# The fourth sum of x later, a PSUM bank for the last token's first half, and one weight remainder made on VectorE

## The chip, the cores and the metric

The kernel runs on one core of a Trainium2 chip. The metric is the device time of one execution in microseconds (us); before the change it is 1440.09 us, the median of three runs from 1439.65 to 1441.46.

## The reference

Two layers of a gated block over 512 tokens of width 1024, in float32. What matters here is the second half of each layer, the SwiGLU:

```python
hn = rmsnorm(x, norm2_g[i])
gate, up = jnp.split(hn @ w_ffn_in[i], 2, axis=-1)      # FFN_HIDDEN = 2816
x = x + (jax.nn.silu(gate) * up) @ w_ffn_out[i]
```

The first half of a layer (one input projection, a pool mixer, differential attention, the output projection) is not changed.

## The kernel before

**Precision by splitting.** Every operand of a product is split into a high part (a cast to float32r on ScalarE, `whi`, `xqh` and so on) and a low part (the value minus the high part, on VectorE: `wlo`, `xql`). A product is three matmuls: high by high (L291 in the SwiGLU), low of x by high of the weight (L293), high of x by low of the weight (L294).

**SwiGLU by seven products.** The 22 blocks of 128 hidden columns are made in eleven pairs (`Ffn(f0)` for f0 = 0, 2, ... 20). A pair needs the product of x (two halves of 512 rows of the width, two halves of 256 tokens) with its gate and up columns, and does it with seven products of quarters instead of eight (`p(n)`, n = 1 to 7, each 24 matmuls of 256 columns). The x side is seven quarters or sums of quarters, made once a layer by `Quarters`: `b11`, `b21`, `b22` are plain quarters, `t1` to `t4` are sums. Of the tiles, `xq` holds b11, b21, b22 and t1, `xr` holds t2 and t3, `xt` holds t4. The sixth product reads t2, the fifth t1, the seventh t3, the third b22, the fourth t4.

**Where the quarters come from.** For each block t of 128 tokens, `normed` makes the normed rows `xs`; `turn` transposes them on TensorE, eight 128x128 blocks, four to a PSUM bank of the pool `tr` (two banks). For t = 0 and 1, `put` copies and splits. For t = 2 and 3 it makes t1 = tvs[0] − r11 (L389), t2 = tvs[1] − t1 (L390), t3 = b22 − tvs[0] (L395) and t4 = r21 − t2 (L398), each with a split (ScalarE's cast L195, VectorE's remainder L196).

**The weight side.** A piece of weights is 128x1024 (512 KB), loaded through SyncE's queue into one of seven `raw` buffers. `parts` splits it. With a piece number it does so without VectorE: ScalarE writes the high part (L233) and −src into the low part (L234), and GpSimd issues a DMA that adds the same weights from memory to it (L235): an accumulating transfer. A pair's sums of weights are made by VectorE in `sums` (L774, L775, L776, L785; `ws` and `raw`).

**The order of the stage.** `ffn_start` takes the first two pairs (`early`): both first products, both second products (while the last two token blocks are transposed), both pairs' `sums`, then `rest` of each: products 6, 5, 7, 3, 4, with the sums on VectorE that put the pieces together (`cqn` L816, `cta` L824, `cpwl` L828, `cal` L830, `cpwh` L836) and `swiglu` (the tanh `th` on ScalarE, L728, its products on VectorE, L729 and L730, then the split into `fh`, `fl`). From the third pair on `ffn_in` does the same for one pair: products 1, 6, 5, 2, 7, 3, 4. The pairs' first and second products gather in a bank of pool `sc`, 6, 7 and 5, 3 in banks of `mm`, the fourth in a bank of `tr`.

The order in which the instructions stand on each engine, and which of a pool's buffers a tile gets, is set when the program is built, by a scheduler that works through the whole program; each engine then runs its instructions in that order. A small edit can so move instructions elsewhere.

Of the kernel before, what the change touches and what calls it, by code (L numbers as in the profile page):

```python
# [22 lines left out]
NT = S // P  # L23
# [84 lines left out]
def trunk_kernel(  # L108
# [12 lines left out]
    nc = tc.nc  # L121
# [10 lines left out]
    def tr_ps():  # L132
        return ps.tile([P, 512], F32, name="tr", tag="tr", bufs=2)

    oy = ps.tile([P, 2, VD], F32, name="oy", tag="oy")
# [57 lines left out]
    def split(hi, lo, src):  # L193

        ins = nc.scalar.copy(hi, src)  # L195
        nc.vector.tensor_sub(lo, src, hi.bitcast(F32))  # L196
        return ins
# [17 lines left out]
    def loaded():  # L215

        i = at[0]
        at[0] += 1
        raw = sb.tile([P, 4, VD], F32, name="raw", tag="raw", bufs=RAWS)
        nc.sync.dma_start(raw.rearrange("p a b -> p (a b)"), wts[i])  # L220
        return i, raw

    def tiles(x):
        return [x[:, k, :] for k in range(x.shape[1])]

    def parts(src, piece_no=None):

        hi = sb.tile([P, 4, VD], F32R, name="whi", tag="whi", bufs=SPLITS)
        lo = sb.tile([P, 4, VD], F32R, name="wlo", tag="wlo", bufs=SPLITS)
        if piece_no is None:  # L230
            split(hi, lo, src)
        else:
            nc.scalar.copy(hi, src)  # L233
            nc.scalar.activation(lo, src, AF.Copy, scale=-1.0)  # L234
            nc.gpsimd.dma_start(lo.rearrange("p a b -> p (a b)"), wts[piece_no], accum_op=ALU.add)  # L235
        return tiles(hi), tiles(lo)
# [23 lines left out]
    def later(delay, what):  # L260
        heapq.heappush(waiting, (clock[0] + delay, count[0], what))
        count[0] += 1
# [36 lines left out]
    def transpose(dst, src):  # L299
        nc.tensor.transpose(dst, src, ident)  # L300
        clock[0] += 2 * P

    def rsqrt_mean(ss, n, width, times=(1.0,), eps=None):

        r = sb.tile([P, width], F32, name="r", tag="r", bufs=4)
        part = width // len(times)
        for i, f in enumerate(times):
            cs = slice(i * part, (i + 1) * part)
            e = EPS / (f * f) if eps is None else eps[i]
            nc.vector.tensor_scalar(r[:, cs], ss[:, cs], 1.0 / (n * f * f), e, op0=ALU.mult, op1=ALU.add)  # L310
        nc.gpsimd.tensor_tensor(r, r, mhalf[:, :width], op=ALU.pow)  # L311
        return r

    def small(name, width=1):
        return sb.tile([P, width], F32, name=name, tag=name, bufs=4)
# [3 lines left out]
    def need(*keys):  # L319
        run_due(lambda: all(k in ready for k in keys))  # L320
# [7 lines left out]
    def normed(key, t, xh, xl, g, into=None):  # L328

        xs = sb.tile([P, D], F32, name="xs", tag="mj", bufs=2)  # L330
        ss = small("ss")
        nc.scalar.activation(xs, res[t], AF.Square, accum_out=ss)
        r = rsqrt_mean(ss, D, 1)
        for half in range(2):
            cs = slice(half * 512, (half + 1) * 512)
            nc.vector.scalar_tensor_tensor(xs[:, cs], res[t][:, cs], r, g[half], op0=ALU.mult, op1=ALU.mult)  # L336

        def turn():
            tvs = []
            for half in range(2):  # L340
                tp = tr_ps()
                for i in range(4):
                    k = half * 4 + i
                    transpose(tp[:, i * P:(i + 1) * P], xs[:, k * P:(k + 1) * P])
                tv = tp.rearrange("p (k c) -> p k c", k=4)
                tvs.append(tv)
                if into is None:
                    ks = slice(half * 4, half * 4 + 4)
                    copied = split(xh[:, ks, t * P:(t + 1) * P], xl[:, ks, t * P:(t + 1) * P], tv)
            if into is not None:  # L350
                copied = into(t, tvs)
            ready.add((key, t))
            return copied

        later(NORM_WAIT, turn)

    class Quarters:


        def __init__(self):  # L360
            four = [sb.tile([P, 4, 4, VD], F32R, name="xq" + p, tag="x" + p) for p in "hl"]
            two = [sb.tile([P, 2, 4, VD], F32R, name="xr" + p, tag="qk", bufs=2) for p in "hl"]
            one = [sb.tile([P, 4, VD], F32R, name="xt" + p, tag="v", bufs=2) for p in "hl"]
            self.b11, self.b21, self.b22, self.t1 = ([x[:, i] for x in four] for i in range(4))
            self.t2, self.t3 = ([x[:, i] for x in two] for i in range(2))
            self.t4 = one
            self.raw = {}

        def put(self, t, tvs):

            cs = slice(t % 2 * P, (t % 2 + 1) * P)

            def out(to, src):
                return split(to[0][:, :, cs], to[1][:, :, cs], src)

            if t < 2:
                for half, to in ((0, self.b11), (1, self.b21)):
                    raw = sb.tile([P, 4, P], F32, name="xw", tag=f"pr{half}", bufs=2)
                    nc.scalar.copy(raw, tvs[half])
                    self.raw[t, half] = raw  # L380
                    last = out(to, raw)
                return last
            r11, r21 = self.raw[t - 2, 0], self.raw[t - 2, 1]

            def temp(tag, bufs):
                return sb.tile([P, 4, P], F32, name="xd", tag=tag, bufs=bufs)

            t1, t2, t3, t4 = temp("us", 2), temp("us", 2), temp("ta", 2), temp("ta", 2)
            nc.vector.tensor_sub(t1, tvs[0], r11)  # L389
            nc.vector.tensor_sub(t2, tvs[1], t1)  # L390
            out(self.t2, t2)
            out(self.t1, t1)
            b22 = temp("up", 2)
            nc.scalar.copy(b22, tvs[1])
            nc.vector.tensor_sub(t3, b22, tvs[0])  # L395
            out(self.b22, b22)
            out(self.t3, t3)
            nc.vector.tensor_sub(t4, r21, t2)  # L398
            return out(self.t4, t4)

    def new_xT():
        xh = sb.tile([P, KD, S], F32R, name="xh", tag="xh")
# [110 lines left out]
    for layer in range(L):  # L513
# [232 lines left out]
        class Ffn:  # L746
# [15 lines left out]
            def gate_in(self, *tags):  # L762
                self.sets[2] = parts_in(self.r12, *tags)

            def sums(self, a12=False):

                _, r21 = loaded()
                n22, r22 = loaded()
                if a12:
                    self.gate_raw(1)  # L770
                s1 = sb.tile([P, 4, VD], F32, name="ws", tag="raw", bufs=RAWS)
                if a12:
                    self.gate(0, self.n11)
                nc.vector.tensor_add(s1, r21, r22)  # L774
                nc.vector.tensor_sub(r21, self.r11, r21)  # L775
                nc.vector.tensor_sub(self.r11, s1, self.r11)  # L776
                self.sets[6] = parts(self.r11)
                if not a12:
                    self.sets[4] = parts(r22, n22)
                self.sets[5] = parts(s1)  # L780
                if a12:
                    self.gate(1, self.n12)
                else:
                    self.sets[7] = parts(r21)
                nc.vector.tensor_sub(self.r12, self.r12, self.r11)  # L785
                if a12:
                    self.sets[7] = parts(r21)
                self.sets[3] = parts(self.r12)
                if a12:
                    self.sets[4] = parts(r22, n22)  # L790
                self.to = hidden_pair(self.f0)
                for i in range(2):
                    hidden[self.f0 + i] = self.to[i]

            def temp(self, tag, bufs=1):
                return sb.tile([P, 2, VD], F32, name="c" + tag, tag=tag, bufs=bufs)
# [42 lines left out]
        quarters, early, last_merged = [], [], []  # L839
# [44 lines left out]
        def ffn_in(f0):  # L884
            x = Ffn(f0)
            x.gate_raw(0)
            x.sums(True)
            x.first()
            x.rest(True)

        def ffn_start():
            need(*((f"h{layer}", t) for t in range(2)))
            for x in early:
                x.first()
            for x in early:
                x.second()
            need(*((f"h{layer}", t) for t in range(2, 4)))
            for x in early:
                x.sums()
            for x in early:  # L900
                x.rest()

# [14 lines left out]
        for r, (f0, f1) in enumerate(ROUNDS):  # L917
            for f in range(f0, f1, 2):
                if f >= 4:
                    ffn_in(f)  # L920
                elif not f:
                    ffn_start()
                if r and f == f0:
                    ffn_out(*ROUNDS[r - 1], False)
# [58 lines left out]
```

## Time and profile before

| | |
|---|---|
| median of three runs | 1440.09 us |
| profiled execution, in all | 1441.58 us |
| its span (first to last instruction) | 1439.8 us |
| TensorE busy | 1428.5 us, 99% |
| VectorE busy | 989.7 us, 69% |
| ScalarE busy | 688.8 us, 48% |
| accumulating transfers (GpSimd's queue) | 62 of 512 KB, median 7.9 us from issue to landing |
| loads of weight pieces (SyncE's queue) | 244 of 512 KB, median 4.3 us |
| granted TensorE clock | 0.999 |

In the profile PE is TensorE, DVE VectorE, ACT ScalarE, POOL GpSimd and SP SyncE. A row of the timeline has the start in us from the span's start, the duration, the engine, the line of the code, the operation, what it writes and reads, and in brackets the engine's idle time before it with what ended it. A row of waits has the waiting instruction, what it waited for, the total in us, how often, and the longest. The first layer's SwiGLU begins near 374 us, the second's about 715 us later. The matmuls of 256 columns start 0.12 us apart; the 0.28 us of their rows overlap.

### The profile page before, as it was taken

The numbers are of one execution on the slowest core, as the hardware profiler recorded it, in microseconds if no ns is written. First come the engines' busy times: TensorE is split into PE (matmuls) and PEld (weight loads), VectorE is DVE, ScalarE is ACT, GpSimd is POOL, SyncE is SP. The second block draws the span as 40 slices with busy tenths as digits, with TensorE's granted clock in tenths as the row PEclk, the third lists the DMA queues.
The fourth block names the chain that finished last, engine by engine and source line by source line (L and its number), as shares of the span: only waits on it lengthen the run. The fifth ranks groups of instructions, "written<-read, shape, count | busy, mean of one in ns | idle before, by whom it ended". The sixth has DMA issues, their size and how long they took to land.

```text
span 1439.8 us, 21587 instructions
## 1 busy us (share of the span) xinstructions
PE 1428.5 (99%) x8375; PEld 1260.5 (88%) x8375; DVE 989.7 (69%) x1837; ACT 688.8 (48%) x1311; POOL 115.2 (8%) x146
## 2 busy tenths in 40 slices
PE   9999999999999999999999999999999999999999
PEld 7878888888999899989888888888889998999897
DVE  7768677677898548737576686665769975587462
ACT  6544343444666346526355443434446662464350
POOL 1010000000011001000010001001000100010000
PEclk9999999999999999999999999999999999999999
DMA  9212231224268357628322132222422783575361
GB/s 361 97 59 70 95 108 59 89 78 120 74 161 208 116 140 176 195 47 236 113 92 78 59 117 79 76 74 73 130 60 79 184 217 107 132 190 163 83 152 59
DMA packets 49782, 173.02 MB, mean 120 GB/s; under 512 B 5648, under 2 KB 6544, under 8 KB 49680
## 3 DMA queue, kind: packets, MB, share of 16 engines
q1 hardware_dynamic: 39456, 137.02, 28.8%
q0 software_dynamic: 8928, 32.51, 12.5%
q10 hardware_dynamic: 1296, 2.11, 0.6%
q8 instruction: 66, 1.08, 0.3%
q14 instruction: 36, 0.29, 0.1%
HBM read 169.52 MB, written 2.10 MB: 119 GB/s over the span
## 4 chain that ended last, share of the span: by engine, by line
PE 91%; issue 3%; DVE 3%; DMA 2%; POOL 0%; ACT 0%; POOLq 0%
PE mm L279 19%; PE mm L281 19%; PE mm L280 19%; PE mm L291 5%; PE mm L293 5%; PE mm L294 5%; PE sc L294 2%; PE sc L293 2%; PE sc L291 2%; PE tr L300 2%; DMA wlo<-in_wts 1%; PE tr L294 1%; PE tr L293 1%; PE tr L291 1%; DVE xs L336 1%
## 5 line engine op out<-in xcount | busy, mean ns | idle before, releaser
L195 ACT CAST whi<-raw 128x1024 fp32r<-128x1024 f32 (+1 forms) x223 | 232.4, 1048 | 206.4 <-issue 118.7
L196 DVE TENSOR_TENSOR wlo<-raw,whi 128x1024 fp32r<-128x1024 f32 (+1 forms) x223 | 269.5, 1215 | 82.0 <-ACT whi L195 79.2
L279 PE MATMUL mm<-whi,xh 128*128 128x512 f32 x480 | 192.4, 401 | 0.0
L281 PE MATMUL mm<-whi,xl 128*128 128x512 f32 x480 | 187.7, 391 | 0.0
L280 PE MATMUL mm<-wlo,xh 128*128 128x512 f32 x480 | 187.4, 390 | 0.0
L718 DVE TENSOR_TENSOR res<-mm,res 128x512 f32<-128x512 f32 (+1 forms) x97 | 65.9, 683 | 116.0 <-PE mm L281 116.0
L281 PE MATMUL mm<-whi,fl 128*128 128x512 f32 (+1 forms) x358 | 138.5, 387 | 0.0
L279 PE MATMUL mm<-whi,fh 128*128 128x512 f32 (+1 forms) x358 | 138.3, 387 | 0.0
L280 PE MATMUL mm<-wlo,fh 128*128 128x512 f32 (+1 forms) x358 | 138.2, 387 | 0.0
L311 POOL TENSOR_TENSOR r<-r,mhalf 128x1 f32<-128x1 f32 (+1 forms) x76 | 59.1, 778 | 635.8 <-DVE r L310 572.9
L281 PEld LDWEIGHTS mm<-whi,xl 128*128 128x128 f32 x480 | 90.1, 188 | 19.5
L279 PEld LDWEIGHTS mm<-whi,xh 128*128 128x128 f32 x480 | 90.2, 188 | 16.8
L280 PEld LDWEIGHTS mm<-wlo,xh 128*128 128x128 f32 x480 | 90.4, 188 | 16.3
L235 POOL DMA_DIRECT2D wlo<-in_wts x62 | 54.3, 877 | 616.1 <-ACT wlo L234 278.0
L279 PE MATMUL mm<-xh,whi 128*128 128x512 f32 x256 | 102.1, 399 | 0.0
L281 PE MATMUL mm<-xh,wlo 128*128 128x512 f32 x256 | 99.9, 390 | 0.0
L291 PE MATMUL mm<-xrh,whi 128*128 128x256 f32 x352 | 99.8, 283 | 0.2
L280 PE MATMUL mm<-xl,whi 128*128 128x512 f32 x256 | 99.8, 390 | 0.0
L293 PE MATMUL mm<-xrl,whi 128*128 128x256 f32 x352 | 99.7, 283 | 0.0
L291 PE MATMUL mm<-xqh,whi 128*128 128x256 f32 x352 | 99.6, 283 | 0.0
L293 PE MATMUL mm<-xql,whi 128*128 128x256 f32 x352 | 99.6, 283 | 0.0
L294 PE MATMUL mm<-xqh,wlo 128*128 128x256 f32 x352 | 99.6, 283 | 0.0
(211 smaller groups left out, 3519.9 us busy)
## 6 DMA issues: line engine op xcount, KB each, us to landing
raw<-in_wts SPq DMA_DIRECT2D x244, 512.0 KB, 4.3
wlo<-in_wts POOLq DMA_DIRECT2D x62, 512.0 KB, 7.9
xr<-in_x_t SPq DMA_DIRECT2D x4, 512.0 KB, 7.7
res<-in_x SPq DMA_DIRECT2D x4, 512.0 KB, 8.7
pwr<-in_pool_w ACTq DMA_DIRECT2D x8, 256.0 KB, 2.7
out<-res SPq DMA_DIRECT2D x7, 256.0 KB, 2.0
g<-in_gains SPq DMA_DIRECT2D x6, 256.0 KB, 3.1
hg<-in_rows SPq DMA_DIRECT2D x4, 128.0 KB, 7.0
```

What stands on the lines that cost most here:

```text
L195: ins = nc.scalar.copy(hi, src)
L196: nc.vector.tensor_sub(lo, src, hi.bitcast(F32))
L235: nc.gpsimd.dma_start(lo.rearrange("p a b -> p (a b)"), wts[piece_no], accum_op=ALU.add)
L279: nc.tensor.matmul(acc, lhsT=ah, rhs=bh, start=i == 0, stop=False)
L280: nc.tensor.matmul(acc, lhsT=ah, rhs=bl, start=False, stop=False)
L281: nc.tensor.matmul(acc, lhsT=al, rhs=bh, start=False, stop=i == n - 1)
L291: nc.tensor.matmul(acc[:, i, :], lhsT=ah, rhs=bh, start=start and not i and not k, stop=False, skip_group_check=True)
L293: nc.tensor.matmul(acc[:, i, :], lhsT=ah, rhs=bl, start=False, stop=False, skip_group_check=True)
L294: last = nc.tensor.matmul(acc[:, i, :], lhsT=al, rhs=bh, start=False, stop=i == 1 and k == 3, skip_group_check=True)
L300: nc.tensor.transpose(dst, src, ident)
L311: nc.gpsimd.tensor_tensor(r, r, mhalf[:, :width], op=ALU.pow)
L718: added = nc.vector.tensor_add(res[t][:, cs], here, res[t][:, cs])
```

## The change

Three edits. The last token block's first four transposes go to `oy`, the bank that attention's output uses otherwise, instead of one of the two `tr` banks (in every norm, so also in the one ahead of layer 2). t4 is no longer made in `put` for each block but in a list of functions that `ffn_start` calls after the first pair's sums; t3 is written over t1, t4 over r21. And the third pair (f0 = 4) alone makes the low part of its fourth weight quarter (r22) on VectorE instead of by an accumulating transfer.

```diff
@@ normed, turn
-                tp = tr_ps()
+                tp = oy.rearrange("p a b -> p (a b)") if t == NT - 1 and not half else tr_ps()
@@ Quarters.put
-            t1, t2, t3, t4 = temp("us", 2), temp("us", 2), temp("ta", 2), temp("ta", 2)
+            t1, t2, b22 = temp("us", 2), temp("up", 2), temp("ta", 2)
             nc.vector.tensor_sub(t1, tvs[0], r11)
             nc.vector.tensor_sub(t2, tvs[1], t1)
             out(self.t2, t2)
             out(self.t1, t1)
-            b22 = temp("up", 2)
             nc.scalar.copy(b22, tvs[1])
-            nc.vector.tensor_sub(t3, b22, tvs[0])
+            nc.vector.tensor_sub(t1, b22, tvs[0])
             out(self.b22, b22)
-            out(self.t3, t3)
-            nc.vector.tensor_sub(t4, r21, t2)
-            return out(self.t4, t4)
+
+            def fourth():
+                nc.vector.tensor_sub(r21, r21, t2)
+                out(self.t4, r21)
+
+            self.fourths.append(fourth)
+            return out(self.t3, t1)
@@ Ffn.sums
-            def sums(self, a12=False):
+            def sums(self, a12=False, by_dma=True):
 ...
                 if a12:
-                    self.sets[4] = parts(r22, n22)
+                    self.sets[4] = parts(r22, n22 if by_dma else None)
@@ ffn_in
-            x.sums(True)
+            x.sums(True, f0 > 4)
@@ ffn_start
-            for x in early:
-                x.sums()
+            early[0].sums()
+            for fourth in quarters[-1].fourths:
+                fourth()
+            early[1].sums()
```

The lines of the changed program are up to four higher than those of before (L390, L391 for L389, L390; L399 for L398; L778 for L774; L834 for L830). What follows shows the order of the two programs at three places; it is the same in both layers, and the rows are those of the first. Numbers behind a name tell tiles apart and differ between the programs.

**VectorE, the last token block.** `xd` are t1, t2, t3 (and t4, before) and the copy of b22; `xrl`, `xql`, `xtl` are the low halves of the split sums. Before, from the second sum of block 2 on:

```order
L196 TENSOR_TENSOR xql_3450<-xd_3683,xqh_3449 128x4x128
L395 TENSOR_TENSOR xd_3685<-xd_3693,tr_3673 128x512
L196 TENSOR_TENSOR xql_3450<-xd_3693,xqh_3449 128x4x128
L398 TENSOR_TENSOR xd_3686<-xw_3582,xd_3684 128x512
L196 TENSOR_TENSOR xrl_3452<-xd_3685,xrh_3451 128x4x128
L389 TENSOR_TENSOR xd_3766<-tr_3756,xw_3629 128x512
L196 TENSOR_TENSOR xtl_3454<-xd_3686,xth_3453 128x4x128
L390 TENSOR_TENSOR xd_3767<-tr_3761,xd_3766 128x512
L196 TENSOR_TENSOR xql_3450<-xd_3766,xqh_3449 128x4x128
L196 TENSOR_TENSOR wlo_3853<-raw_3831,whi_3852 128x1024
L196 TENSOR_TENSOR xrl_3452<-xd_3767,xrh_3451 128x4x128
```

Now:

```order
L196 TENSOR_TENSOR xql_3450<-xd_3683,xqh_3449 128x4x128
L196 TENSOR_TENSOR wlo_3842<-raw_3820,whi_3841 128x1024
L395 TENSOR_TENSOR xd_3683<-xd_3685,tr_3673 128x512
L196 TENSOR_TENSOR xql_3450<-xd_3685,xqh_3449 128x4x128
L390 TENSOR_TENSOR xd_3760<-oy_64,xw_3629 128x512
L196 TENSOR_TENSOR xrl_3452<-xd_3683,xrh_3451 128x4x128
L391 TENSOR_TENSOR xd_3761<-tr_3755,xd_3760 128x512
L196 TENSOR_TENSOR xql_3450<-xd_3760,xqh_3449 128x4x128
L196 TENSOR_TENSOR wlo_3847<-raw_3463,whi_3846 128x1024
L196 TENSOR_TENSOR xrl_3452<-xd_3761,xrh_3451 128x4x128
```

The two fourth-sum operations (L398 and xtl) have gone behind the last row, and two weight splits instead of one stand ahead of it.

**VectorE and ScalarE, while TensorE does the first pair's last products.** `cal` is the first pair's sum behind its third product, `th` its tanh tiles; `whi_4206`/`wlo_4207` (now `whi_4201`/`wlo_4202`) are the two parts of the third pair's first weight quarter, which goes by an accumulating transfer. VectorE before:

```order
L830 TENSOR_TENSOR cal_4001<-mm_3896,cqn_3921 128x512
L196 TENSOR_TENSOR wlo_3881<-ws_3867,whi_3880 128x1024
L196 TENSOR_TENSOR wlo_3885<-raw_3863,whi_3884 128x1024
L196 TENSOR_TENSOR wlo_3890<-raw_3465,whi_3889 128x1024
L729 SCALAR_TENSOR_TENSOR th_4003<-th_4003,cal_4001 128x512
```

Now:

```order
L196 TENSOR_TENSOR wlo_3876<-ws_3862,whi_3875 128x1024
L196 TENSOR_TENSOR wlo_3880<-raw_3858,whi_3879 128x1024
L196 TENSOR_TENSOR wlo_3885<-raw_3465,whi_3884 128x1024
L834 TENSOR_TENSOR cal_3996<-mm_3891,cqn_3916 128x512
L840 TENSOR_TENSOR cpwh_4031<-tr_4006,cta_3968 128x512
L778 TENSOR_TENSOR ws_4200<-raw_4194,raw_4196 128x1024
L733 SCALAR_TENSOR_TENSOR th_3998<-th_3998,cal_3996 128x512
L733 SCALAR_TENSOR_TENSOR th_4033<-th_4033,sc_3669 128x512
```

and next after it:

```order
L734 SCALAR_TENSOR_TENSOR th_3998<-th_3998,cpwl_3994 128x512
L734 SCALAR_TENSOR_TENSOR th_4033<-th_4033,cpwh_4031 128x512
L196 TENSOR_TENSOR fl_3851<-th_3998,fh_3850 128x256 x2
L196 TENSOR_TENSOR fl_3851<-th_4033,fh_3850 128x256 x2
L820 TENSOR_TENSOR cqn_4067<-mm_4041,cqn_3746 128x512
```

`cal` has moved from ahead of three weight splits to behind them, and the second pair's adder (L820, L816 before) stands behind the third pair's `ws` and all of the first pair's `th` work. ScalarE before:

```order
L728 ACTIVATE th_4003<-cal_4001 128x512
L728 ACTIVATE th_4038<-sc_3669 128x512
L233 CAST whi_4206<-raw_4197 128x1024
L234 ACTIVATE wlo_4207<-raw_4197 128x1024
L195 CAST fh_3861<-th_4003 128x256 x2
```

Now:

```order
L233 CAST whi_4201<-raw_4192 128x1024
L732 ACTIVATE th_3998<-cal_3996 128x512
L732 ACTIVATE th_4033<-sc_3669 128x512
L234 ACTIVATE wlo_4202<-raw_4192 128x1024
L195 CAST fh_3850<-th_3998 128x256 x2
```

The cast of the high part has gone ahead of the two tanh; the −src pass, behind which the transfer is issued, is still behind them, and so behind `cal`.

**TensorE, between the second pair's fifth product (`mm_4047`, now `mm_4042`) and its seventh.** `sc_4245` (now `sc_4239`) is the third pair's first product. Before:

```order
L294 MATMUL mm_4047<-xqh_3449,wlo_3881 128x256
L291 MATMUL sc_4245<-xqh_3449,whi_4206 128x256
L291 MATMUL mm_4046<-xrh_3451,whi_3884 128x256
L293 MATMUL mm_4046<-xrl_3452,whi_3884 128x256
L294 MATMUL mm_4046<-xrh_3451,wlo_3885 128x256
```

Now:

```order
L294 MATMUL mm_4042<-xqh_3449,wlo_3876 128x256
L291 MATMUL sc_4239<-xqh_3449,whi_4201 128x256
L293 MATMUL sc_4239<-xql_3450,whi_4201 128x256
L294 MATMUL sc_4239<-xqh_3449,wlo_4202 128x256
L291 MATMUL sc_4239<-xqh_3449,whi_4201 128x256
L293 MATMUL sc_4239<-xql_3450,whi_4201 128x256
L291 MATMUL mm_4041<-xrh_3451,whi_3879 128x256
```

Five matmuls of the third pair's first product now stand where one stood, and the third of the five reads the low part.

More of the change, by code (lines that the diff above doesn't have):

```diff
@@ L367, in __init__ @@
             self.raw = {}
+            self.fourths = []
         def put(self, t, tvs):
```

## The prediction

> **What bounds the kernel now.** I read the page's busy shares and chain first, then TensorE's waits, then the rows around each wait that the change touches.
>
> ```profile
> PE 1428.5 (99%) x8375; PEld 1260.5 (88%) x8375; DVE 989.7 (69%) x1837; ACT 688.8 (48%) x1311; POOL 115.2 (8%) x146
> ...
> PE 91%; issue 3%; DVE 3%; DMA 2%; POOL 0%; ACT 0%; POOLq 0%
> ```
>
> TensorE is busy for 99% of the span and carries 91% of the chain. So the time moves only where TensorE stands still, and a new standstill is paid in full. Its waits, all of the program but two at its very start (total, times, longest):
>
> ```profile
> PE tr L294 <- DMA wlo<-in_wts: 2.5, 2, 1.4
> ...
> PE oy L279 <- DVE mt L586: 1.1, 1, 1.1
> PE tr L300 <- DVE xd L395: 0.9, 2, 0.6
> PE tr L300 <- DVE ql L196: 0.3, 1, 0.3
> PE tr L300 <- DVE xl L196: 0.2, 1, 0.2
> ```
>
> Two rows belong to the change, each once a layer: the last token's transposes wait for L395, and the third pair's fourth product waits for an accumulating transfer. Together they are 3.4 us, and nothing else here is to be gained. TensorE's rows at these places, the first layer's and then the second's (start, duration):
>
> ```profile
> 382.66 0.66 PE L300 MATMUL tr<-ident,xs 128*128 128x128 f32 x4 [0.57 <-DVE xd L395]
> ...
> 388.54 0.28 PE L291 MATMUL mm<-xrh,whi 128*128 128x256 f32 x1
> ...
> 403.04 0.28 PE L293 MATMUL tr<-xtl,whi 128*128 128x256 f32 x1
> ...
> 409.04 0.28 PE L291 MATMUL sc<-xqh,whi 128*128 128x256 f32 x1
> 409.16 0.28 PE L291 MATMUL mm<-xrh,whi 128*128 128x256 f32 x1
> ...
> 417.92 0.28 PE L294 MATMUL sc<-xqh,wlo 128*128 128x256 f32 x1
> ...
> 436.76 0.39 PE L294 MATMUL tr<-xth,wlo 128*128 128x256 f32 x1 [1.40 <-DMA wlo<-in_wts]
> ...
> 1097.41 0.66 PE L300 MATMUL tr<-ident,xs 128*128 128x128 f32 x4 [0.32 <-DVE xd L395]
> ...
> 1103.30 0.28 PE L291 MATMUL mm<-xrh,whi 128*128 128x256 f32 x1
> ...
> 1123.80 0.28 PE L291 MATMUL sc<-xqh,whi 128*128 128x256 f32 x1
> ...
> 1151.44 0.39 PE L294 MATMUL tr<-xth,wlo 128*128 128x256 f32 x1 [1.12 <-DMA wlo<-in_wts]
> ```
>
> The reader is to see the single matmul at 409.04. It is the first of the third pair's first product, set by the scheduler between the second pair's fifth and seventh products. It needs the weight's high half alone; the low half is first read at 417.92, almost 9 us later.
>
> **Part 1, the transposes' own bank (and the fourth sum moved).** The waits of 0.57 and 0.32 us go: the first half needs no transpose bank, the second takes the bank that is free early. What is late next is the sixth product, which starts at 388.54 and needs the last token's second sum split (xrl). VectorE's rows ahead of it:
>
> ```profile
> 381.32 0.68 DVE L196 TENSOR_TENSOR xql<-xd,xqh 128x512 fp32r<-128x512 f32 x1
> 381.93 0.68 DVE L395 TENSOR_TENSOR xd<-xd,tr 128x512 f32<-128x512 f32 x1
> ...
> 386.73 1.22 DVE L196 TENSOR_TENSOR wlo<-raw,whi 128x1024 fp32r<-128x1024 f32 x1
> 387.86 0.68 DVE L196 TENSOR_TENSOR xrl<-xd,xrh 128x512 fp32r<-128x512 f32 x1
> ```
>
> That split ends at 388.54, the instant the sixth product starts, so there is no slack. In the new order there stand, between the rows of 381.32 and 387.86, six operations of 512 columns (0.60 us from start to start) and two weight splits of 1024 (1.13), where there were eight and one. With the 0.61 of the first step that is 6.47 us instead of 6.54. The fourth sum and its split went behind, but a weight split took their place. So the sixth product can start 0.07 us earlier and no more; TensorE gets there half a microsecond early and waits for xrl instead. The bounds are 0 and the 0.57 and 0.32 us whole; I take 0.07 a layer, since VectorE runs through this stretch with no idle time in these rows. The second layer is as tight (1103.30) and gets the same. The moved fourth sums cost nothing: the first pair's fourth product, which reads them, starts 24 matmuls of 0.12 us before 403.04 + 0.24, at 400.4, and by the new order the last of their splits is the eighth operation behind xrl: six of 0.60 and one of 1.13 come between, so it ends near 393.8.
>
> **Part 2, the third pair's fourth remainder on VectorE.** It removes one accumulating transfer a layer and the waits of 1.40 and 1.12 us. It adds one 1024-column split (1.14 us) on VectorE, and ScalarE loses its second pass. The new split stands just ahead of the sum behind the third pair's sixth product:
>
> ```profile
> 425.88 0.68 DVE L816 TENSOR_TENSOR cqn<-mm,cqn 128x512 f32<-128x512 f32 x1
> ```
>
> TensorE asks for it at 436.76 − 1.40 = 435.4, over 9 us later, so it is hidden; were that cover gone it would cost its 1.14 us a layer. Below nothing too: both waits gone is all it can give. I take 1.40 + 1.12 whole.
>
> **Part 3, what the moved order does between, and it decides.** In the changed program five matmuls of the third pair's first product, not one, stand ahead of the second pair's seventh product. The third of them reads the low half, wlo, which comes by an accumulating transfer. TensorE works in order, as the row at 409.04 shows, so it stands there until that transfer has landed. It asks at 409.04 + 0.24 − 0.07 = 409.2, and at 1124.0 in the second layer. When is the transfer issued? Behind ScalarE's pass that writes −src into wlo, and that pass now stands behind the two tanh of the first pair, the first of which needs cal (L830):
>
> ```profile
> 399.71 1.03 ACT L195 CAST whi<-ws 128x1024 fp32r<-128x1024 f32 x1
> 400.65 1.99 ACT L195 CAST whi<-raw 128x1024 fp32r<-128x1024 f32 x2
> 402.55 0.63 ACT L728 ACTIVATE th<-cal 128x512 f32<-128x512 f32 x1
> 403.08 0.58 ACT L728 ACTIVATE th<-sc 128x512 f32<-128x512 f32 x1
> 403.56 1.04 ACT L233 CAST whi<-raw 128x1024 fp32r<-128x1024 f32 x1
> 404.49 1.06 ACT L234 ACTIVATE wlo<-raw 128x1024 fp32r<-128x1024 f32 x1
> ```
>
> ```profile
> 400.61 0.69 DVE L830 TENSOR_TENSOR cal<-mm,cqn 128x512 f32<-128x512 f32 x1
> 401.21 1.22 DVE L196 TENSOR_TENSOR wlo<-ws,whi 128x1024 fp32r<-128x1024 f32 x1
> ...
> 404.62 0.69 DVE L729 SCALAR_TENSOR_TENSOR th<-th,cal 128x512 f32<-128x512 f32 x1
> ```
>
> cal was ahead of three splits and is now behind them. The first split waits for ScalarE's cast, over at 399.71 + 1.03 = 400.7; the three take 404.62 − 401.21 = 3.4 us; cal runs from 404.1 to 404.8. The cast of whi, now ahead of the tanh, waits for the fourth product's last high-half matmul (403.04) and is done by then. The tanh take 403.56 − 402.55 = 1.0 us, the −src pass 1.06: over at 406.9, where it was over at 405.55. The transfers' issues and landings, for GpSimd's queue:
>
> ```profile
> 405.91 0.87 POOL L235 DMA_DIRECT2D wlo<-in_wts  x1 [4.83 <-DVE cpwh L836]
> ```
>
> ```profile
> DMA to landing us min/median/max: 8.2/8.2/8.2
> ```
>
> ```profile
> 1120.71 0.86 POOL L235 DMA_DIRECT2D wlo<-in_wts  x1 [4.85 <-DVE cpwh L836]
> ```
>
> ```profile
> DMA to landing us min/median/max: 7.0/7.0/7.0
> ```
>
> ```profile
> DMA to landing us min/median/max: 5.4/7.9/10.4
> ```
>
> The first landing row is that transfer's in layer 1 (405.91 + 8.2 = 414.1), the second the same in layer 2 (1127.7), the last that of all 62. The issue is 0.36 behind the pass, so it comes at 407.25, 1.35 later than before; in layer 2 at 1122.05. If the transfer keeps its duration it lands at 415.45 and 1129.0, and TensorE stands for 6.2 and 5.0 us. If the traffic around it sets its end (the third pair's weight loads, and the accumulating transfer of the second pair's fourth product, are still under way in both programs), it lands when it did before, at 414.1 and 1127.7: 4.9 and 3.7 us. I take a point nearer to the second in layer 1, 414.3, since it queues there anyway, and the middle in layer 2, 1128.4: 5.1 + 4.4 = 9.5 us. As outer ends I keep the fastest of the 62, 5.4 us (3.4 + 3.4 = 6.8), and the slowest, 10.4 us (8.4 + 8.4 = 16.8).
>
> A second new wait hides under it. The adder L816, which frees the bank for the second pair's seventh product, ran at 408.29:
>
> ```profile
> 408.29 0.68 DVE L816 TENSOR_TENSOR cqn<-mm,cqn 128x512 f32<-128x512 f32 x1
> 408.89 0.75 DVE L196 TENSOR_TENSOR fl<-th,fh 128x256 fp32r<-128x256 f32 x2
> 409.56 1.22 DVE L774 TENSOR_TENSOR ws<-raw 128x1024 f32<-128x1024 f32 x1
> ```
>
> It now stands behind all that these rows show, the third pair's ws sum and all four splits of the hidden blocks (0.67 for two). From cal at 404.1: cal, cpwh, ws, four operations on th, four splits, that is 0.60 + 0.60 + 1.14 + 2.40 + 1.34 = 6.1 us, and its own 0.68: it ends near 410.9, where TensorE would come at 409.04 + 5 × 0.12 − 0.07 = 409.6. That is 1.3 us a layer, paid only if the transfer were quick.
>
> The Trainium skill, "DMA: Bandwidth & Descriptors", section "Anatomy of one DMA — SWDGE (gpsimd) path", gives a transfer from GpSimd's queue about 2.0 us plus its bytes at 436 GB/s, an estimate of 3.2 us for 512 KB; by it TensorE would be freed at 410.5, the adder's 1.3 us a layer would be what is left, and the sum would come to about nothing. The trace does not agree: the shortest of its 62 transfers took 5.4 us.
>
> **The sum.** +9.5 − 2.52 − 0.14 = +6.8 us; by the outer ends +4.1 and +14.1. TensorE has no later wait in either layer's remainder that could give it back. The profiled execution took 1439.8 us of span and 1441.58 in all, 1.5 above the median of the three runs, 1440.09; the difference is added to the median: 1446.9.
>
> **The rivals.**
> - A quick transfer, no change. If the low half lands within 3.3 us of its issue (by 410.6, so that its three matmuls are over when the adder is), only the adder's 1.3 us a layer is left against 2.65 gained: 1440.1. The transfer ahead of it has then to be out of the way, and the fastest of the 62 took 5.4. Chance 0.05. It is what the Trainium skill's sum of the paragraph above would make of it.
> - Faster. The low half is there when TensorE asks: landed by 409.2, that is 2.0 us after its issue, and VectorE is 1.3 us ahead of my walk at the adder. Then all four waits of before are saved, at best 3.4 us: 1436.7. That xrl is on time to the instant speaks against the first 0.9 us of it. It decides at a landing of 2.0 us. Chance 0.03.
> - Slower still. Both transfers meet the traffic that the slowest met, 10.4 us: +14.1, 1454.2. For it: the transfer issued just ahead shares the queue; against: the load transfers beside it start a little earlier than before, not later. Chance 0.08.
> - That the low half was to come by VectorE here too, and the wait doesn't exist, is excluded: the third pair's first quarter still goes by the transfer.
>
> **The numbers.** The forecast, landings from 5.4 us to 9 us after the issue, has 0.84. Its ends are 1444.2 (both at 5.4) and about 1450.7 (some 9 us and 8 us: stalls of 7.2 and 6.1). That is the range; it leaves out 0.16. A measurement of this kernel tells 0.2%, 2.9 us, from no change. Faster by more 0.03, within 0.05, slower 0.92.
>
> **What would show it.** Right: a new row of TensorE, sc <- DMA wlo, twice, 3.7 to 6.2 us each, near 414 and 1128; the rows tr <- DMA wlo and tr <- xd L395 gone; a short wait of TensorE for xrl near 388.5; the transfer's issue near 407.3. Wrong: no such row, or one below 1.5 us; a tr wait that stays in the third pair; or VectorE's waits growing behind the standstill, so that later products wait as well.

## The result, and the profile after

The changed kernel took 1448.97 us, the median of 6 executions (1446.67 to 1452.83), where the kernel before took 1439.88 beside it (6 executions, 1439.58 to 1442.33). The ratio is 1.0064, with a 95% interval of 1.0047 to 1.0081: slower by some 9 us. The forecast was 1446.9, with a range of 1444.2 to 1450.7. The profiled execution took 1449.7 us, its span 1447.9, 8.1 more than before.

The page's first part and its chain:

```profile
PE 1430.7 (99%) x8375; PEld 1263.5 (87%) x8375; DVE 991.4 (68%) x1839; ACT 690.2 (48%) x1309; POOL 113.6 (8%) x144
...
PE 93%; issue 3%; DVE 3%; DMA 1%; POOL 0%; ACT 0%; POOLq 0%
```

TensorE's share of the chain rose, and its busy time by 2.2 us, though it has the same 8375 matmuls. That is the first hint of something beside waits: the same work took longer. TensorE's waits in the changed kernel (total, times, longest):

```profile
PE sc L294 <- DMA wlo<-in_wts: 6.0, 2, 3.0
PE mm L291 <- DVE cqn L820: 2.6, 2, 1.3
...
PE mm L293 <- DVE xrl L196: 0.8, 2, 0.5
```

Both old rows (tr<-DMA wlo and tr<-xd L395) are gone, and three new ones have come. In TensorE's rows, layer by layer:

```profile
388.46 0.39 PE L293 MATMUL mm<-xrl,whi 128*128 128x256 f32 x1 [0.49 <-DVE xrl L196]
...
395.64 0.36 PE L291 MATMUL mm<-xrh,whi 128*128 128x256 f32 x1 [1.29 <-DVE cqn L820]
...
410.11 0.28 PE L291 MATMUL sc<-xqh,whi 128*128 128x256 f32 x1
410.23 0.28 PE L293 MATMUL sc<-xql,whi 128*128 128x256 f32 x1
413.44 0.52 PE L294 MATMUL sc<-xqh,wlo 128*128 128x256 f32 x1 [2.93 <-DMA wlo<-in_wts]
...
1132.13 0.36 PE L294 MATMUL sc<-xqh,wlo 128*128 128x256 f32 x1 [3.05 <-DMA wlo<-in_wts]
```

The third matmul of the third pair's first product is where TensorE stands. Idle times in brackets are modelled; what each place cost is read better from starts. Both traces hold 8375 matmuls. Number them in the order in which they start: the start of the n-th one after, less that of the n-th before, stays level over long stretches and steps where time is lost or won. Each entry is such a step:

| place | first layer, us | second layer, us |
|---|---|---|
| last token's transposes (own bank) | -0.77 | -0.54 |
| sixth product, waits for xrl | +0.71 | +0.49 |
| first pair's seventh product, waits for adder L820 | +1.20 | +1.18 |
| third pair's first product, its third matmul waits for wlo | +3.09 | +3.21 |
| the matmuls right behind it | +1.57 | +1.54 |
| third pair, second and fourth products | -1.65 | -0.20 and -1.38 |
| transposes that end the first layer | -0.40 | |

With steps under 0.1 us this comes to +8.08. The row "right behind it" is no wait. Stretches of this trace (duration, busy time of each engine with its instructions, then the granted clock of TensorE, the DMA share and GB/s):

```profile
410.06:413.47 3.41, 0.48 (x5) 0.31 (x4) 3.06 (x4) 0.82 (x2) 0.00 (x0) 1.00 0.70 132
413.47:416.88 3.41, 3.41 (x16) 3.41 (x17) 0.00 (x0) 1.76 (x2) 0.00 (x0) 0.50 0.00 0
416.88:420.30 3.42, 3.42 (x31) 3.42 (x30) 1.86 (x3) 1.94 (x2) 0.00 (x0) 1.00 0.02 5
...
1126.86:1130.27 3.41, 2.23 (x19) 2.02 (x17) 3.41 (x7) 1.91 (x5) 0.45 (x1) 1.00 1.03 251
1130.27:1133.69 3.42, 1.56 (x13) 1.59 (x14) 1.45 (x2) 1.85 (x2) 0.00 (x0) 1.00 0.29 58
1133.69:1137.10 3.41, 3.41 (x18) 3.41 (x18) 0.06 (x1) 0.38 (x2) 0.00 (x0) 0.50 0.00 0
```

Behind each standstill the granted clock is 0.50 for 3.41 us: 16 matmuls fall into 413.47 to 416.88, 31 into the next stretch of the same length (those that only reach into a stretch are counted too). In the trace of before the clock is 1.00 from the warm-up to the kernel's last 2 us.

### The profile page after: what moved, and what is told of

Its sections match the earlier page's. It is cut to its first block, busy times and chain, and to the rows that moved or that the text cites. A ratio compares the mean times of both kernels' runs of the same rounds, so it can differ in the third digit from the quotient of the medians.

```text
span 1447.9 us, 21585 instructions
## 1 busy us (share of the span) xinstructions
PE 1430.7 (99%) x8375; PEld 1263.5 (87%) x8375; DVE 991.4 (68%) x1839; ACT 690.2 (48%) x1309; POOL 113.6 (8%) x144
## 4 chain that ended last, share of the span: by engine, by line
PE 93%; issue 3%; DVE 3%; DMA 1%; POOL 0%; ACT 0%; POOLq 0%
PE mm L279 19%; PE mm L281 19%; PE mm L280 19%; PE mm L293 5%; PE mm L294 5%; PE mm L291 5%; PE sc L294 2%; PE tr L300 2%; PE sc L293 2%; PE sc L291 2%; PE tr L294 1%; PE tr L293 1%; PE tr L291 1%; DMA wlo<-in_wts 1%; PE sc L281 1%
## 5 line engine op out<-in xcount | busy, mean ns | idle before, releaser
L294 PE MATMUL mm<-xrh,wlo 128*128 128x256 f32 x352 | 100.8, 286 | 0.0
```

The lines of the kernel that those rows point to most:

```text
L294: last = nc.tensor.matmul(acc[:, i, :], lhsT=al, rhs=bh, start=False, stop=i == 1 and k == 3, skip_group_check=True)
```

## The experiments

The theory after the result: the moved fourth sums alone cause the loss. By them the scheduler sets five matmuls of the third pair's first product early, where they meet a late transfer, and sets the first pair's adder late. The rivals: the bank's early transposes, or VectorE's added split, cause it. In what follows "by starts" is the comparison of the table above, each profiled execution against that of before.

**The bank alone.** Against the kernel before:

```
-                tp = tr_ps()
+                tp = oy.rearrange("p a b -> p (a b)") if t == NT - 1 and not half else tr_ps()
```

> The kernel before with the last token's own bank alone. Theory: the transposes' waits of 0.57 and 0.32 us for L395 go, but the sixth product gets its xrl no earlier (VectorE's order there is unchanged), so TensorE waits 0.5 and 0.3 us for xrl instead and the time stays within 0.3 us of before (ratio 1.000), with no clock below 1.0 inside the kernel. Rival (the bank's early transposes are what moved the order): the early rows sc<-DMA wlo appear here and the time is 5 us or more above before. Second rival (the gain is real): 0.9 us below.

Measured: 1441.04 us beside 1440.79, ratio 0.9999 (0.9990 to 1.0007). The waits for L395 are gone, and one for xrl has come:

```profile
PE mm L293 <- DVE xrl L196: 0.9, 2, 0.6
PE tr L294 <- DMA wlo<-in_wts: 0.3, 1, 0.3
```

By starts the transposes won 0.79 and 0.54 us, and the sixth product gave back 0.80 and 0.55. There is no early sc row. So the bank is not at fault and is worth next to nothing. The second row was not expected: the wait for the third pair's transfer shrank though nothing about it was changed. In this execution the full clock came 5.6 us later at the start, and TensorE's work was some 1.8 us late from there on. The first layer's transfer landed only 0.3 us later (437.0 against 436.7), so TensorE met it with 1.3 us less to wait.

**The third pair's remainder alone.** Against the kernel before:

```
...
-                    self.sets[4] = parts(r22, n22)
+                    self.sets[4] = parts(r22, n22 if by_dma else None)
...
-            x.sums(True)
+            x.sums(True, f0 > 4)
```

> The kernel before with the third pair's fourth remainder on VectorE alone. Theory: the two waits of TensorE for the accumulating transfer (1.4 and 1.1 us, 1.5 by starts) go and nothing comes in their place: 2.5 us below before, ratio 0.998. Rival (the added 1.1 us split a layer on VectorE is what makes the later products late): a VectorE wait of TensorE behind 425 us, and no gain or a loss.

Measured: 1438.33 us beside 1440.79, ratio 0.9986 (0.9977 to 0.9995). By starts 1.6 and 1.4 us were won at the third pair's fourth product, and nothing was lost. The rival falls: no wait for VectorE comes behind 425 us.

**The moved fourth sums alone.** Against the kernel before, with the buffers of the change:

```
...
-            nc.vector.tensor_sub(t4, r21, t2)
-            return out(self.t4, t4)
+            def fourth():
+                nc.vector.tensor_sub(r21, r21, t2)
+                out(self.t4, r21)
+            self.fourths.append(fourth)
+            return out(self.t3, t1)
...
+            early[0].sums()
+            for fourth in quarters[-1].fourths:
+                fourth()
+            early[1].sums()
```

> The kernel before with the moved fourth sums (and their buffers) alone. Theory: all the loss is here. TensorE waits for the adder of the first pair 1.3 us a layer and for the low half of the third pair's first quarter 2.9 us a layer, the granted clock falls to 0.5 for 3.4 us after each of the two standstills, and the waits for L395 stay: 9 to 11 us above before if the fourth quarter's transfer of the third pair is then on time (TensorE comes later), up to 13 if it still makes TensorE wait. Rivals (bank or third pair's remainder at fault): within 1 us of before.

Measured: 1450.57 us beside 1440.79, ratio 1.0068 (1.0055 to 1.0081): about as much as the whole change lost. Its waits:

```profile
PE sc L294 <- DMA wlo<-in_wts: 6.0, 2, 3.2
PE tr L300 <- DVE xd L395: 2.5, 2, 1.4
...
PE mm L291 <- DVE cqn L820: 0.9, 2, 0.5
```

By starts: 0.8 and 0.8 at the transposes, whose wait for L395 has grown, 0.4 and 0.4 at the adder (1.3 expected, but TensorE had lost 0.8 just ahead of it), 3.0 and 3.35 at wlo, 1.5 and 2.5 at half clock. The third pair's wait for its fourth transfer, 1.4 and 1.1 us before, is gone here as well, without the edit that removes the transfer: by starts -1.65 and -1.38. TensorE comes 5 us or more late there, and no wait for the transfer is left.

**The changed kernel, third pair's first product held back.**

```
-                    self.p(4, d)
+                    fourth = self.p(4, d)
...
-                x.rest()
+                behind[:] = [x.rest()]
...
+                with tc.issue_after(behind[0].ins):
+                    x.first()
```

> The changed kernel with one more condition: the third pair's first product may not start before the second pair's last one is issued. Theory: the standstills for the low half go and with them the half clock (about 9 us in all); left are the waits for the two adders, 1.3 us a layer in the first pair and about 1.0 a layer in the second, xrl 0.8, against 3.4 saved: 1442, 2 us above before. Rival (the first product meets its transfer late wherever it stands, or VectorE's lateness is the cause): a wait of several us for wlo or for VectorE stays near 415 to 420 and the time stays above 1446.

Measured: 1441.85 us beside 1440.79, ratio 1.0009 (1.0000 to 1.0018). TensorE's longest row now:

```profile
PE mm L291 <- DVE cqn L820: 3.9, 4, 1.3
```

No wait for wlo and no half clock are left: the changed kernel without the five early matmuls is 7 to 8 us quicker (7.1 by the medians; by starts, less 1.6 us of a later full clock at the start, it is 0.3 above before instead of 8.08). The first pair's adder costs 1.2 us a layer by starts, the second pair's 0.9.

**The changed kernel, that low half from VectorE too.**

```
-                    self.gate(0, self.n11)
+                    self.gate(0, self.n11 if by_dma else None)
```

> The changed kernel with the low half of the third pair's first quarter made on VectorE as well, so that no accumulating transfer is waited for; nine matmuls of that product are early. Theory: the two standstills of 3 us and the two stretches of half clock (9.3 us by starts) go; the added split of 1.14 us a layer pushes the second pair's adder back, and TensorE waits for it 0.5 to 1.5 us a layer: 1441 to 1443. Rival (VectorE has no room at this place): a wait of 3 us or more for VectorE at the early matmuls or the adder takes the transfer's place, and the time stays above 1446.

Measured: 1440.12 us beside 1440.66, ratio 0.9996 (0.9987 to 1.0005), a little better than expected. Nine matmuls stand early here, and none waits:

```profile
PE mm L291 <- DVE cqn L820: 2.6, 2, 1.3
```

These are the first pair's two waits alone (1.2 each by starts). The rival's wait of 3 us for VectorE did not come. The early matmuls are harmless when their data are there; they even cover the second pair's adder. The late transfer is what made them costly.

**The changed kernel, fourth sums ahead of the first pair's sums.**

```
-            early[0].sums()
             for fourth in quarters[-1].fourths:
                 fourth()
+            early[0].sums()
             early[1].sums()
```

> The changed kernel with the moved fourth sums made just ahead of the first pair's sums instead of between the two pairs' sums; all three edits stay. Only one matmul of the third pair's first product is then early, as before. Theory: both new standstills and the half clock go, the adder of the first pair is on time again, the third pair's gain of about 2.8 us by starts stays, and so does 0.4 us of the bank's at the layer's end; at the sixth product nothing or up to 0.8 a layer: 1436.5 to 1437.7, ratio 0.997 to 0.998, no sc<-DMA wlo row. Rival (the bank's early transposes or the changed buffers cost something too): cqn or xrl waits remain and it is no faster than the third pair's edit alone (1438.3).

Measured: 1439.40 us beside 1440.66, ratio 0.9987 (0.9978 to 0.9995). Both standstills are gone with the place of one call, though the buffers are those of the change: so it is the place, and neither the buffers nor the moving as such, that made the standstills. But the median lies above the expected 1436.5 to 1437.7, and it is no faster than the third pair's edit alone; there the rival was right. At the sixth product nothing is lost any more, but 0.81 and 0.55 us are at the next one, all of the 0.80 and 0.54 won at the transposes. TensorE arrives early and waits for the operations that read its accumulators:

```profile
PE mm L291 <- DVE cqn L820: 0.9, 1, 0.9
PE mm L291 <- ACT cah L823: 0.6, 1, 0.6
```

Five of the eleven executions lie at 1437.7 to 1438.2 and six at 1439.4 to 1440.2. The profiled one is of the upper group and had the late full clock at its start, 1.6 us (last section).

**The bank and the third pair's remainder, nothing moved** (both first diffs together).

> The kernel before with the bank and the third pair's remainder, the fourth sums where they were. Theory (the moved sums alone lose): the two gains add up, 2.8 to 3.2 us of the third pair's and 0.5 of the bank's: 1436.8 to 1437.4 where before has 1440.5, ratio 0.9975, no wlo and no cqn wait. Rival (the edits need each other, and the bank without the moved sums disturbs the third pair): no better than the third pair's edit alone, 0.9986.

Measured: 1439.24 us beside 1440.18, ratio 0.9992 (0.9983 to 1.0001). The median lies above the expected 1436.8 to 1437.4. By starts it won 3.69 us, as the theory has it, but against a profiled execution of before that took 1441.58 us, 1.4 us more than before's median beside these runs. The third pair's 1.6 and 1.4 us are among them, so the bank does not disturb the third pair, and no wait for wlo or the adder is left. The executions lie in two groups, five at 1437.8 to 1438.1 and six at 1439.2 to 1439.8; the profiled one is of the lower group and had the early full clock at its start. A late full clock (last section) would explain the upper group; the runs without a profile do not show it. Whether it beats the third pair's edit alone is not told by these runs.

**The late transfer in two halves**, to see what the clock depends on. The changed kernel again, with only the third pair's first quarter handled otherwise, in a branch of `parts`:

```
+        elif isinstance(piece_no, tuple):
...
+            for h in range(2):
+                nc.gpsimd.dma_start(lo[:, 2 * h:2 * h + 2, :].rearrange("p a b -> p (a b)"),
+                                    wts[piece_no][:, h * 512:(h + 1) * 512], accum_op=ALU.add)
...
-                    self.gate(0, self.n11)
+                    self.gate(0, self.n11 if by_dma else (self.n11,))
```

> The changed kernel with the late accumulating transfer of the third pair's first quarter issued as two of 256 KB; the scheduler then sets nine matmuls early, the third reading the first half, the ninth the second. Theory (the clock falls since TensorE stands still for 3 us at a stretch): the wait is cut into two, the first near 2 us, the second below 2, no record of clock 0.5 inside the kernel, and about 3 us less than the changed kernel: 1444 to 1446. Rival (the total idle time of the stretch counts, or the fall belongs to the place): clock 0.5 for 3.4 us here too and 1447.5 or more. If both halves land together, as late as the whole did, the wait stays 3 us and the two say the same.

Measured: 1449.83 us (1445.96 to 1452.28) beside 1440.66, ratio 1.0061 (1.0048 to 1.0075), no better than the change. Its profiled execution was the fastest, 1445.96, and did what the theory said: four waits of 0.5 to 1.8 us, no half clock. In the first layer:

```profile
408.41:411.82 3.41, 2.26 (x19) 2.09 (x18) 3.41 (x7) 1.78 (x5) 1.18 (x2) 1.00 0.99 219
411.82:415.24 3.42, 2.06 (x16) 1.86 (x17) 1.32 (x2) 1.97 (x2) 0.00 (x0) 1.00 0.33 53
415.24:418.65 3.41, 3.41 (x31) 3.41 (x30) 1.39 (x2) 1.50 (x3) 0.00 (x0) 1.00 0.02 5
```

The other executions had mean clocks down to 0.996. So the same program was run and profiled twice more.

> The kernel of the two halves once more, to see the clock's records of another execution: its profiled execution had no half clock and a mean clock of 0.999, while other executions had 0.996 to 0.997. If the phase of something that runs freely decides, some executions of this same program show 0.5 for one or more stretches of 3.4 us behind the two short waits, others none, with the same waits of 1 to 2 us; if the length of a single wait decides, no execution shows it here.

> As the run ahead of it, a third look at the same program: 0.5 behind waits of under 2 us in at least one of the looks if the phase decides, in none if the length of a single wait does.

Measured: 1448.83 and 1450.24 us. The waits are much the same, 4.7 and 4.8 us in four beside 4.8 in the first profile, none over 1.6 us. In the first of the two the clock fell in layer 1 and not in layer 2:

```profile
412.25:415.67 3.42, 1.48 (x10) 1.31 (x11) 2.25 (x2) 1.11 (x3) 0.00 (x0) 1.00 0.50 80
415.67:419.08 3.41, 3.41 (x18) 3.41 (x17) 0.00 (x0) 0.96 (x2) 0.00 (x0) 0.50 0.00 0
...
1129.05:1132.47 3.42, 1.82 (x16) 1.65 (x14) 3.39 (x6) 0.78 (x2) 0.21 (x1) 1.00 0.93 147
1132.47:1135.88 3.41, 2.61 (x22) 2.40 (x21) 0.34 (x1) 2.00 (x2) 0.00 (x0) 1.00 0.09 16
```

In the last it fell in both, for 6.8 and 3.4 us. The theory that one wait of 3 us is needed falls: the same program with much the same waits shows both. What decides is where the waits fall in a grid of time that the program does not set (last section).

## Why the prediction was right, step by step

The sign, the mechanism and the order of size were right, and the median lies in the range. But that the total came out only 2 us off is luck, since two misses cancelled: 3.2 us too much at the transfer, 5.5 us not foreseen. The measured standstill, 6.3 us, lies below even the prediction's outer end of 6.8. Without the 5.5 us the kernel would have come to about 1442.7, below the range.

- **Part 3, the standstill**: right in kind, mis-sized, 9.5 us forecast and 3.09 + 3.21 = 6.3 measured; each of the two is below the 3.7 to 6.2 us that were to show it. TensorE asked 1.1 us later than forecast (the adder, below), and the transfer was quick. The transfer and the one ahead of it on GpSimd's queue, with the time to landing of the two, before and then after:

```profile
400.17 0.92 POOL L235 DMA_DIRECT2D wlo<-in_wts  x1 [20.82 <-ACT wlo L234]
405.91 0.87 POOL L235 DMA_DIRECT2D wlo<-in_wts  x1 [4.83 <-DVE cpwh L836]
...
DMA to landing us min/median/max: 8.2/8.6/9.1
```

```profile
399.98 0.92 POOL L235 DMA_DIRECT2D wlo<-in_wts  x1 [20.69 <-ACT wlo L234]
407.80 0.88 POOL L235 DMA_DIRECT2D wlo<-in_wts  x1 [6.91 <-DVE th L733]
...
DMA to landing us min/median/max: 5.5/6.8/8.2
```

  The issue was forecast at 407.25. The landing took 5.5 us in layer 1 and 5.6 in layer 2, where it had taken 8.2 and 7.0 before: issued 1.9 us later than before, it landed 0.8 us sooner, at 413.3. Of the two ways in which the prediction bounded it, the one in which the traffic sets the end was the nearer one, and the outer end of 5.4 us nearer still. What set the end can be read from the rows: before, the transfer ahead landed at 400.17 + 9.1 = 409.2, 3.3 us behind this one's issue; now at 399.98 + 8.2 = 408.2, 0.4 behind it. Wherever this quarter came by one whole transfer, in eight traces and both layers, it landed 4.5 to 5.5 us behind the landing of the one ahead of it, while the time from its own issue went from 5.4 to 8.2. No run moved the one ahead alone. The Trainium skill's sum of 3.2 us ("DMA: Bandwidth & Descriptors", section "Anatomy of one DMA — SWDGE (gpsimd) path") is not borne out here either.
- **Part 3, the second pair's adder**: right that it hides under the standstill. Its price without that cover, forecast 1.3 us a layer, was 0.9 with the product held back, and 0 where nine matmuls without a wait stood ahead of it.
- **Part 1, "the moved fourth sums cost nothing"**: this step failed. It followed the fourth sums to their reader, and that reader was on time. It did not follow what the new order of VectorE put ahead of the first pair's adder. Before, and then after:

```profile
392.61 1.22 DVE L774 TENSOR_TENSOR ws<-raw 128x1024 f32<-128x1024 f32 x1
393.75 0.68 DVE L816 TENSOR_TENSOR cqn<-mm,cqn 128x512 f32<-128x512 f32 x1
394.35 1.21 DVE L775 TENSOR_TENSOR raw<-raw 128x1024 f32<-128x1024 f32 x1
```

```profile
393.06 0.69 DVE L196 TENSOR_TENSOR xtl<-xw,xth 128x512 fp32r<-128x512 f32 x1
393.67 1.23 DVE L779 TENSOR_TENSOR raw<-raw 128x1024 f32<-128x1024 f32 x1
394.80 0.69 DVE L820 TENSOR_TENSOR cqn<-mm,cqn 128x512 f32<-128x512 f32 x1
```

  The adder (L816, now L820) has changed places with one sum of 1024 columns (L775, now L779), 1.13 us, at a place where TensorE waited for it to the instant already: 1.2 us a layer, 2.4 in all. With the fourth sums ahead of the first pair's sums this price is gone: what TensorE loses at the adder there is only what it won at the transposes.
- **Part 1, the bank**: right that xrl takes the place of the transposes' wait; -0.06 and -0.05 measured, -0.07 each forecast. Not seen: the same bank serves the transposes that end the first layer, 0.40 us.
- **Part 2**: right, -2.52 forecast and -3.0 by starts in the run of this edit alone (-2.5 by its medians). But the run of the moved sums alone shows that in the changed kernel the edit is not what saves it: a TensorE that is 5 us late doesn't meet this wait anyhow.
- **The half clock**, +3.1 us: not in the prediction at all. It bounded the standstill by its own length.

## What to carry to other kernels

When an operation is moved, look at every place where the consumer waits to the instant already, and read what stands ahead of that producer in the new order, not only whether the moved results are in time. A matmul that a scheduler sets early is free only if all its operands, the slow transfers among them, are due by then; here the place of one call, before or behind the first pair's sums, decided some 10 us (1448.97 against 1439.40). A standstill of TensorE can cost more than its length: here each step of half clock behind one added 1.5 us, in some executions and not in others, so expect times that scatter from run to run.

## What the runs showed of the hardware

- The clock falls by a grid of 3.413 us that runs on from the start. After its warm-up the changed kernel's clock was full from 3.87 us, and it fell at 413.47 and 1133.68: 120 and 331 steps of 3.413 later. The other profiled executions with such a fall keep the same step, each with a phase of its own.
- What counts is TensorE's busy time within one step. With 0.48, 1.16, 1.40, 1.48 and 1.56 us of 3.41 the next step ran at 0.50; with 1.82, 2.06, 2.23 and 2.26 it did not. Over all steps at full clock in the twelve traces there is no exception: behind each of the 19 with 1.56 us or less the clock was 0.50, behind none with 1.61 or more. So a standstill of 3 us can be enough and one of 2 us may be, by where it falls in the grid, and two short ones in one step add up. A step at half clock costs 1.5 us. When TensorE was busy for only 2.23 or 2.80 us of such a step, the next was at half clock too. The Trainium skill ("TensorE: Matmul & The Clock Gate", section "HAM oscillation — how this bites in real kernels") has the rule of no idle gap over about 3.4 us, and its section "What's actually happening" a free-running window of that length. The window agrees with these traces; the length of the gap does not, since waits under 2 us were enough here.
- The full clock came at 3.9 to 5.6 us in some profiled executions and at 9.5 to 10.2 in others, and all matmuls behind the start were then 1.4 to 1.8 us later, by starts. The times of five kernels (the third pair's edit alone, the product held back, the low half from VectorE, the fourth sums ahead, the two edits with nothing moved) fall into two groups some 1.6 us apart, and each of the five profiled executions lies in the group that its start gives it. For the executions without a profile the link is argued only. Before and the bank alone show no such groups: a late TensorE waits less for the third pair's transfer there (the bank's trace). A part of a microsecond is not told from the medians of such runs; the comparison by starts tells it, for the one execution that each trace holds.
